# Broadcasting the roots for the keys' normalization in a fused decoder layer: through DRAM in place of a diagonal times ones

## The chip, the cores and the metric

The kernel runs on one core of a Trainium2 chip. The metric is the device time of one execution in microseconds (us), lower is better. A core has five engines with a queue of instructions each: TensorE (PE, matmuls, with its weight loads shown apart as PEld), VectorE (DVE), ScalarE (ACT), GpSimd (POOL) and SyncE (SP), which here only issues DMAs. An engine runs its queue in order and waits for others by semaphores.

## What is computed

One hybrid decoder layer on 1024 tokens with 1024 channels: RMS norm, one projection, sliding-window attention beside retention, an output projection, and a feed-forward part with a convolution. What matters here is the beginning, cut from the reference:

```python
def rms_norm(x, w):
    xf = x.astype(jnp.float32)
    y = xf * lax.rsqrt(jnp.mean(xf * xf, axis=-1, keepdims=True) + RMS_EPS)
    return (y * w.astype(jnp.float32)).astype(x.dtype)
...
        h = rms_norm(x, mix_pre_norm[l])
        proj = jnp.einsum('bsd,de->bse', h, w_in[l])
        q_a, k_a, v_a, q_r, k_r, v_r, g_r = jnp.split(proj, splits, axis=-1)
        attn_out = sliding_window_sink_attention(q_a, k_a, v_a, attn_sinks[l])
        ret_out = retention_group(q_r, k_r, v_r, g_r)
```

The kernel projects the input without dividing it by its root mean square, and brings the factor of each token in afterwards. For most products this factor is a column (tokens lie on partitions). The keys of the attention lie the other way: 128 key channels on the partitions, 512 tokens along the row. For them the factors of 512 tokens are needed as a row, repeated on all 128 partitions.

## The kernel before

The tokens are worked in two halves of 512 (`hh` = 0 and 1). The matmuls take float32 operands as a sum of two reduced parts, `hi` and `lo`: `split` (L114) makes `hi` on ACT (L118, tiles `oh_...`) and `lo` on DVE (L119, tiles `ol_...`), and `mm3` (L125) issues three matmuls for each product: L127 with `hi`, L128 with the other operand's `lo`, L129 with the weights' `lo`. The weights come by `load_w` (L109), a DMA in SP's queue into one of three buffers, so that a load waits until DVE has split the load three before it.

A half begins with `prepare`, which loads and splits the input, and then runs a list of units (L529 to L532): `q_unit` for the four blocks of queries, with `half_sums` between them (loads of the tokens as rows, `mixa` and `mixr`, squared and summed by ACT), `setup`, `k_unit` for the keys, and four `nat_unit` for values. `setup` calls `half_stats`, which computes the roots: a sum on DVE (`v_pre`, L144), the power -1/2 on POOL (`r_pre`, L146), and a few scaled copies on DVE. It then loads constants and tables: in the first half `rm`, `nsink`, `rc`, `cvp`, and in both `cs` and `sn`. In the second half the units stand interleaved with the retention of the first half (tiles `pO`, `pV`, `pI`, `pK`, `inn`, `knat`, `gnt`).

`k_unit` multiplies the keys' weights with the input into `ps_k` (24 matmuls), makes the repeated row `bs`, and multiplies `ps_k` by it into `kn`, which is then split into `kkh` and `kkl`. The row is made in `broadcast`: DVE multiplies the identity by each of the four columns of roots (`diag`, L152), PE multiplies a matrix of ones by that (`bc`, L156, in float32), and ACT copies the result out of PSUM (`bs`, L230).

The order on each engine is set when the program is built, by a scheduler that places instructions by their dependencies and its own estimates; `in_turn` fixes it for a few buffers. A pool hands out buffers in turn by tag: `ttile` is a pool of five (`bs`, `kn`, `sw`, `inn`, `knat`, `gnt`, `th`, `ao` use it), and whoever takes a buffer waits for the last reader of the tile that had it.

Of the kernel before, what the change touches and what calls it, by code (L numbers as in the profile page):

```python
# [8 lines left out]
F32 = mybir.dt.float32  # L9
F32R = mybir.dt.float32r  # L10
AF = mybir.ActivationFunctionType
ALU = mybir.AluOpType
AX = mybir.AxisListType

P = 128
# [12 lines left out]
def tile_hymba_layer(  # L28
# [18 lines left out]
    nc = tc.nc  # L47
# [5 lines left out]
    dr = ctx.enter_context(tc.tile_pool(name="dr", bufs=1, space=bass.MemoryType.DRAM))  # L53
# [4 lines left out]
    def small(name):  # L58
        return pss.tile([P, H], F32, tag="psm", name=name)
# [7 lines left out]
    def xtile(name):  # L67
        return g.tile([P, H], F32, tag="fx", name=name, bufs=2)

    def const(name, shape):  # L70
        return g.tile(shape, F32, tag=name, name=name)

    ident = const("ident", [P, P])
    make_identity(nc, ident)
    ones = const("ones", [P, P])
# [14 lines left out]
    cvp = const("cvp", [P, 2 * NF, 4])  # L90
    nsink = const("nsink", [P, 8])
    rc = const("rc", [P, 3, 4])
    x1d = dr.tile([2, P, D], F32, name="x1d")
    yd = dr.tile([NF, P, D], F32, name="yd")
    ud = dr.tile([EARLY, P, D], F32, name="ud")
# [36 lines left out]
    def block(src, act, name):  # L132
        ops = split_w(src, 1024, H, name) if isinstance(src, bass.AP) else src
        ps = big(f"ps_{name}")
        ah, al = act
        for k in range(8):
            hi, lo = ops[k // 4]
            ks = slice(k % 4 * P, k % 4 * P + P)
            mm3(ps, hi[:, ks], lo[:, ks], ah[k // 4][:, k % 4, :], al[k // 4][:, k % 4, :], k == 0, k == 7)
        return ps  # L140

    def rms(ss, n, name):
        v = g.tile([P, n], F32, tag="cv", name=f"v_{name}", bufs=4)
        nc.vector.tensor_scalar(out=v, in0=ss, scalar1=1.0 / D, scalar2=EPS, op0=ALU.mult, op1=ALU.add)  # L144
        r = g.tile([P, n], F32, tag="cr", name=f"r_{name}", bufs=4)
        nc.gpsimd.tensor_tensor(out=r, in0=v, in1=mhalf[:, :n], op=ALU.pow)  # L146
        return v, r

    def broadcast(r, name):
        diag = xtile(f"diag_{name}")  # L150
        for b in range(4):
            nc.vector.tensor_scalar(  # L152
                out=diag[:, b * P : b * P + P], in0=ident, scalar1=r[:, b : b + 1], scalar2=None, op0=ALU.mult
            )
        bc = small(f"bc_{name}")
        nc.tensor.matmul(bc, ones, diag, start=True, stop=True)  # L156
        return bc


    mixer = ExitStack()  # L160
    m = mixer.enter_context(tc.tile_pool(name="m", bufs=1, reuse_waits="tile"))
# [1 line left out]
    def ttile(name, dt=F32):  # L163
        return m.tile([P, H], dt, tag="t", name=name, bufs=5)
# [3 lines left out]
        out=tri, in_=ones, pattern=[[-1, P]], compare_op=ALU.is_ge, fill=0.0, base=0, channel_multiplier=1  # L168
# [34 lines left out]
    def half_stats(hh, st):  # L203
        ss = st["ss"]
        v, r = rms(ss, 4, f"pre{hh}")
        r8 = m.tile([P, 4], F32, tag="r8", name=f"r8_{hh}", bufs=2)
        nc.vector.tensor_scalar(out=r8, in0=r, scalar1=0.125, scalar2=None, op0=ALU.mult)
        rh = m.tile([P, 4], F32, tag="rh", name=f"rh_{hh}", bufs=2)
        nc.vector.tensor_scalar(out=rh, in0=r, scalar1=0.5, scalar2=None, op0=ALU.mult)
        r2 = m.tile([P, 4], F32, tag="r2", name=f"r2_{hh}", bufs=2)  # L210
        nc.vector.tensor_tensor(out=r2, in0=r, in1=r, op=ALU.mult)
        nr8 = m.tile([P, 4], F32, tag="nr8", name=f"nr8_{hh}", bufs=2)
        nc.vector.tensor_scalar(out=nr8, in0=r, scalar1=-0.125, scalar2=None, op0=ALU.mult)
        return v, r, r8, rh, r2, nr8

    def q_unit(hh, j, act, st):
# [8 lines left out]

    def k_unit(hh, act, st):
        ps = block(w_inT[4], act, f"k{hh}")
        bc = broadcast(st["cols"][1], f"pre{hh}")
        bs = ttile(f"bs{hh}")
        nc.scalar.activation(bs, bc, AF.Copy)  # L230
        kn = ttile(f"kn{hh}")
        nc.vector.tensor_tensor(out=kn, in0=ps, in1=bs, op=ALU.mult)
        cs = slice(P, P + H)
        if hh == 1:
            for t in (kkh, kkl):
                nc.scalar.activation(t[:, :, 0:P], t[:, :, H : H + P].bitcast(F32), AF.Copy)
        for gi in range(2):
            own = slice(gi * 64, gi * 64 + 64)
            oth = slice(64 - gi * 64, 128 - gi * 64)
            for o in (own, oth):  # L240
                nc.scalar.activation(kkh[o, gi, cs], kn[own, :], AF.Copy)
            for o in (own, oth):
                nc.vector.tensor_tensor(
                    out=kkl[o, gi, cs], in0=kn[own, :], in1=kkh[own, gi, cs].bitcast(F32), op=ALU.subtract
                )
# [262 lines left out]
    for hh in range(2):  # L508
        act, w0 = prepare(hh)
        st = dict(w0=w0, q1={}, rq={}, rk={}, va=va_all, vr={}, gp={}, s={}, p={}, ik={}, t={})  # L510
        stages.append(st)
        cs = m.tile([P, H], F32, tag="cs", name=f"cs{hh}")
        sn = m.tile([P, H], F32, tag="sn", name=f"sn{hh}")
        st["rot"] = (cs, sn)
        st["mixa"] = atile(f"mixa{hh}", F32)
        st["mixr"] = atile(f"mixr{hh}", F32)

        def setup(hh=hh, st=st, cs=cs, sn=sn):
            st["cols"] = half_stats(hh, st)
            if hh == 0:  # L520
                nc.sync.dma_start(rm, rmask)
                nc.sync.dma_start(nsink, sinks)
                nc.vector.tensor_scalar(out=nsink, in0=nsink, scalar1=-1.0, scalar2=None, op0=ALU.mult)
                nc.sync.dma_start(rc, rcols)
                nc.sync.dma_start(cvp, convp)
            nc.sync.dma_start(cs, rot[0, hh])
            nc.sync.dma_start(sn, rot[1, hh])

        first = [(q_unit, hh, 0, act, st), (q_unit, hh, 1, act, st), (half_sums, hh, st, (0, 1))]  # L529
        first += [(q_unit, hh, 2, act, st), (half_sums, hh, st, (2, 3)), (q_unit, hh, 3, act, st), (setup,)]  # L530
        first += [(k_unit, hh, act, st)]
        first += [(nat_unit, hh, 0, kk, act, st) for kk in range(4)]  # L532
        interleave(first, prev)
        second = [(rot_unit, hh, t, h, act, st) for t in range(2) for h in range(4)]
        second += [(nat_unit, hh, w, kk, act, st) for w in (1, 2) for kk in range(4)]
        interleave(second, att_stages(hh, st), 0.95)
        prev = ret_stages(hh, st)
# [136 lines left out]
    for hh in range(2):  # L674
        ha, la = split_mix(hh, "mixa", "ma")
        hr, lr = split_mix(hh, "mixr", "mr")
        st = dict(m={})
        st_out.append(st)
        main = [(out_unit, hh, dh, kk, ((ha, hr), (la, lr)), st) for dh in range(2) for kk in range(4)]
        if hh == 0:  # L680
            interleave(main, prev, 0.85)
            mixer.close()
            f = ctx.enter_context(tc.tile_pool(name="ffn", bufs=1, reuse_waits="tile"))
# [536 lines left out]
```

## Time and profile before

| | before |
|---|---|
| runs, median (lowest to highest) | 1061.22 us (1060.53 to 1061.4), 3 runs |
| the profiled execution, its own time | 1060.87 us |
| its span in the trace | 1059.2 us |
| granted TensorE clock, mean | 0.997 |
| instructions | 14259 |
| PE busy | 1047.8 us |
| DVE busy | 820.7 us |
| ACT busy | 592.4 us |
| POOL busy | 111.0 us |
| DMA moved | 149.67 MB |

The span reaches from the first to the last instruction in the trace; what lies around it is 1.7 us. Times in the timelines count from the start of the span. A line names the engine, the line of the kernel, the operation and the tiles, written before read, with the buffers' numbers left out; SPq marks a DMA issue in SP's queue. The sum of busy times is far above the span because the engines work beside each other.

### The profile page before, as it was taken

The page shows a single profiled execution, that of the slowest core. Times are in us where ns is not written, and L with a number is a line of the kernel's source. Part 1 is how long each engine was busy: PE and PEld are TensorE (multiplying, and loading weights), DVE is VectorE, ACT ScalarE, POOL GpSimd, SP SyncE. Part 2 cuts the span into 40 slices and gives each one's busy share as a digit, 9 for nine tenths or more (in the row PEclk, how much of TensorE's full clock was granted, in tenths as well). Part 3 has the DMA queues.
Part 4 walks back from the last instruction along what each step waited for, and adds up shares of the span by engine and source line. Part 5 has one row for each costly group of instructions (what it writes and reads, how often), then busy time and mean ns, then how long its engine had stood idle before and what let it go on. Part 6 is the DMA issues. An engine that isn't in the chain of part 4 may idle for free.

```text
span 1059.2 us, 14259 instructions
## 1 busy us (share of the span) xinstructions
PE 1047.8 (99%) x5004; PEld 887.9 (84%) x5004; DVE 820.7 (77%) x1416; ACT 592.4 (56%) x1140; POOL 111.0 (10%) x135
## 2 busy tenths in 40 slices
PE   9999999999999999999999999999999999999996
PEld 7988998988998888888888888888888888888885
DVE  5567777667686685987787888978879898858695
ACT  7566772466662567665555455555555545445461
POOL 1013332124322110000000000000000000000032
PEclk9999999999999999999999999999999999999998
DMA  8322541222231473864423234233233695604576
GB/s 317 114 80 68 172 174 46 95 80 61 65 108 53 166 251 107 297 213 149 139 86 123 100 110 139 95 114 113 97 140 109 239 338 173 231 33 163 180 195 118
DMA packets 53928, 149.67 MB, mean 141 GB/s; under 512 B 6368, under 2 KB 6496, under 8 KB 53856
## 3 DMA queue, kind: packets, MB, share of 16 engines
q1 hardware_dynamic: 51840, 145.09, 39.8%
q0 software_dynamic: 1728, 3.15, 2.0%
q8 instruction: 39, 0.64, 0.2%
q10 hardware_dynamic: 288, 0.52, 0.1%
q14 instruction: 33, 0.27, 0.1%
HBM read 123.05 MB, written 25.69 MB: 140 GB/s over the span
## 4 chain that ended last, share of the span: by engine, by line
issue 57%; PE 37%; DVE 2%; POOL 1%; DMA 1%; ACT 1%; DVEq 0%; POOLq 0%; ACTq 0%
PE pn L129 3%; PE pn L127 3%; PE pn L128 3%; PE ps_r L127 3%; PE ps_r L128 3%; PE ps_r L129 3%; PE po L127 2%; PE po L129 2%; PE po L128 2%; PE ps_q L128 1%; PE ps_q L129 1%; PE ps_q L127 1%; PE pS L319 1%; PE pS L318 1%; PE pI L395 1%
## 5 line engine op out<-in xcount | busy, mean ns | idle before, releaser
L127 PE MATMUL pd<-oh_d,sh_d 128*128 128x512 f32 x264 | 103.8, 393 | 0.0
L128 PE MATMUL pd<-ol_d,sh_d 128*128 128x512 f32 x264 | 103.2, 391 | 0.0
L129 PE MATMUL pd<-oh_d,sl_d 128*128 128x512 f32 x264 | 103.0, 390 | 0.0
L710 DVE SCALAR_TENSOR_TENSOR a<-uv,cvp,a 128x1023 f32<-128x1023 f32 (+1 forms) x44 | 56.2, 1278 | 22.1 <-ACT a L707 22.1
L1013 POOL TENSOR_TENSOR fs<-fs,mhalf 128x1 f32<-128x1 f32 x8 | 8.3, 1039 | 594.0 <-DVE fs L1010 594.0
L127 PE MATMUL pn<-oh_n,xh 128*128 128x384 f32 x192 | 65.9, 343 | 0.0
L129 PE MATMUL pn<-oh_n,xl 128*128 128x384 f32 x192 | 64.4, 336 | 0.0
L128 PE MATMUL pn<-ol_n,xh 128*128 128x384 f32 x192 | 64.3, 335 | 0.0
L129 PEld LDWEIGHTS pd<-oh_d,sl_d 128*128 128x128 f32 x264 | 49.6, 188 | 11.3
L127 PEld LDWEIGHTS pd<-oh_d,sh_d 128*128 128x128 f32 x264 | 49.6, 188 | 10.9 <-DVE ug L872 0.2
L128 PEld LDWEIGHTS pd<-ol_d,sh_d 128*128 128x128 f32 x264 | 49.6, 188 | 10.4
L710 DVE SCALAR_TENSOR_TENSOR a<-ug,cvp,a 128x1023 f32<-128x1023 f32 (+1 forms) x44 | 56.3, 1279 | 1.2 <-ACT a L707 1.1
L127 PE MATMUL ps_r<-xh,oh_r 128*128 128x512 f32 x128 | 50.6, 396 | 0.0
L128 PE MATMUL ps_r<-xl,oh_r 128*128 128x512 f32 x128 | 50.0, 391 | 0.0
L129 PE MATMUL ps_r<-xh,ol_r 128*128 128x512 f32 x128 | 50.0, 390 | 0.0
L336 ACT ACTIVATE s<-s,sc,r 128x128 f32<-128x128 f32 x64 | 30.9, 483 | 30.2 <-DVE sc L330 30.2
L118 ACT ACTIVATE oh_n<-wr_n 128x384 fp32r<-128x384 f32 x48 | 24.2, 521 | 30.0 <-PE ps_q L128 8.6
L118 ACT ACTIVATE oh_o<-wr_o 128x512 fp32r<-128x512 f32 x32 | 20.0, 635 | 34.2 <-PE po L129 32.9
L707 ACT ACTIVATE a<-ug,cvp 128x1024 f32<-128x1024 f32 x22 | 27.3, 1241 | 19.3 <-DVE ug L872 15.3
L744 DVE TENSOR_TENSOR raw<-raw 128x512 f32<-128x512 f32 x22 | 15.2, 689 | 28.4 <-DMA raw<-w_u 28.4
L718 ACT ACTIVATE sh_d<-r 128x512 fp32r<-128x512 f32 x33 | 20.7, 629 | 28.6 <-PE pd L128 21.9
L119 DVE TENSOR_TENSOR ol_o<-wr_o,oh_o 128x512 fp32r<-128x512 f32 x32 | 23.1, 732 | 17.3 <-ACT oh_o L118 17.2
(1248 smaller groups left out, 3289.0 us busy)
## 6 DMA issues: line engine op xcount, KB each, us to landing
raw<-w_u SPq DMA_DIRECT2D x44, 512.0 KB, 4.4
yd<-a SPq DMA_DIRECT2D x22, 512.0 KB, 2.9
r<-yd SPq DMA_DIRECT2D x22, 512.0 KB, 5.5
wr_n<-w_inN SPq DMA_DIRECT2D x24, 384.0 KB, 3.1
wr_r<-w_inT SPq DMA_DIRECT2D x16, 512.0 KB, 3.4
wr_o<-w_o SPq DMA_DIRECT2D x16, 512.0 KB, 3.4
wr_e<-w_u SPq DMA_DIRECT2D x11, 512.0 KB, 4.4
ud<-e SPq DMA_DIRECT2D x11, 512.0 KB, 3.9
```

Of the source, the lines that this page charges most:

```text
L118: in_turn("oh", nc.scalar.activation(hi[:, :n], src, AF.Copy))
L119: nc.vector.tensor_tensor(out=lo[:, :n], in0=src, in1=hi[:, :n].bitcast(F32), op=ALU.subtract)
L127: ins = nc.tensor.matmul(ps, lh, rh, start=first, stop=False, skip_group_check=onto)
L128: nc.tensor.matmul(ps, lh, rl, start=False, stop=False, skip_group_check=onto)
L129: nc.tensor.matmul(ps, ll, rh, start=False, stop=end, skip_group_check=onto)
L318: nc.tensor.matmul(ps[:, i, :nk], lq, kkh[:, gi, k0 : k0 + nk], start=True, stop=False)
L319: nc.tensor.matmul(ps[:, i, :nk], lq, kkl[:, gi, k0 : k0 + nk], start=False, stop=True)
L336: nc.scalar.activation(s[:, i, :], s[:, i, :], AF.Exp, scale=r8, bias=c[:, 1, i : i + 1], accum_out=c[:, 3, i : i + 1])
L707: nc.scalar.activation(a, u[:, c0 : c0 + n], AF.Identity, scale=cvp[:, b, 2:3], bias=cvp[:, b, 3:4])
L710: nc.vector.scalar_tensor_tensor(out=a[:, s:], in0=u[:, c0 + s - d : c0 + n - d], scalar=cvp[:, b, tap : tap + 1], in1=a[:, s:], op0=ALU.m ...
L718: in_turn("sh", nc.scalar.activation(hi, src, AF.Copy))
L744: nc.vector.tensor_tensor(out=a11, in0=a11, in1=a21, op=ALU.subtract)
```

## The change

The repeated row is no longer made by DVE, PE and ACT. `half_stats` sends the roots (128 partitions with 4 columns each) to a new DRAM tile `rd` by a DMA that writes element by element, so that `rd` holds 4 x 128 numbers in the tokens' order, and a second DMA reads these 512 numbers back to each of the 128 partitions, into `bs`. Both are issued from SP. The second waits until the first has landed. `broadcast` goes, with its matrix product; `k_unit` takes `bs` as it finds it. `bs` is taken from the pool of five earlier, in `setup`.

```diff
@@ -90,6 +90,7 @@
     rc = const("rc", [P, 3, 4])
+    rd = dr.tile([2, 4, P], F32, name="rd")
     x1d = dr.tile([2, P, D], F32, name="x1d")
@@ -145,16 +146,6 @@
-    def broadcast(r, name):
-        diag = xtile(f"diag_{name}")
-        for b in range(4):
-            nc.vector.tensor_scalar(
-                out=diag[:, b * P : b * P + P], in0=ident, scalar1=r[:, b : b + 1], scalar2=None, op0=ALU.mult
-            )
-        bc = small(f"bc_{name}")
-        nc.tensor.matmul(bc, ones, diag, start=True, stop=True)
-        return bc
@@ -211,6 +202,9 @@
         nc.vector.tensor_scalar(out=nr8, in0=r, scalar1=-0.125, scalar2=None, op0=ALU.mult)
+        nc.sync.dma_start(rd[hh].rearrange("b p -> p b"), r)
+        st["bs"] = ttile(f"bs{hh}")
+        nc.sync.dma_start(st["bs"], rd[hh].rearrange("b p -> (b p)").partition_broadcast(P))
         return v, r, r8, rh, r2, nr8
@@ -225,9 +219,7 @@
         ps = block(w_inT[4], act, f"k{hh}")
-        bc = broadcast(st["cols"][1], f"pre{hh}")
-        bs = ttile(f"bs{hh}")
-        nc.scalar.activation(bs, bc, AF.Copy)
+        bs = st["bs"]
         kn = ttile(f"kn{hh}")
```

What the scheduler makes of it is seen in the order of instructions. SP's queue in the first half, before (loads of constants and tables, then of the weights of the keys, `wr_k`, and of the values, `wr_n`):

```order
L524 DMA rc<-rcols 128x12
L525 DMA cvp<-convp 128x176
L526 DMA cs_153<-rot 128x512
L527 DMA sn_154<-rot 128x512
L112 DMA wr_k_339<-w_inT 128x1024
L112 DMA wr_n_0_0_397<-w_inN 128x768
```

and now:

```order
L516 DMA rc<-rcols 128x12
L205 DMA rd<-r_pre_323 128x4x1
L517 DMA cvp<-convp 128x176
L518 DMA cs_154<-rot 128x512
L519 DMA sn_155<-rot 128x512
L207 DMA bs_334<-rd 128x512
L113 DMA wr_k_343<-w_inT 128x1024
L113 DMA wr_n_0_0_392<-w_inN 128x768
```

The write of the roots stands ahead of three loads, and the read back ahead of `wr_k`; nothing else in this stretch of the queue has changed its place.

SP's queue in the second half, at the same units, before:

```order
L200 DMA mixr_1622<-xN 128x1024 x2
L112 DMA wr_k_1968<-w_inT 128x1024
L112 DMA wr_n_0_0_2042<-w_inN 128x768
L112 DMA wr_n_0_1_2082<-w_inN 128x768
L112 DMA wr_n_0_2_2155<-w_inN 128x768
L112 DMA wr_n_0_3_2195<-w_inN 128x768
```

and now:

```order
L191 DMA mixr_1617<-xN 128x1024 x2
L113 DMA wr_k_1966<-w_inT 128x1024
L113 DMA wr_n_0_0_2031<-w_inN 128x768
L205 DMA rd<-r_pre_1912 128x4x1
L113 DMA wr_n_0_1_2071<-w_inN 128x768
L113 DMA wr_n_0_2_2144<-w_inN 128x768
L207 DMA bs_1923<-rd 128x512
L113 DMA wr_n_0_3_2184<-w_inN 128x768
```

Here both stand behind `wr_k`, among the loads for the values.

PE at the end of the keys' block in the first half, before (`ps_k` keys, `bc` the product of ones and the diagonal, `pn` values):

```order
L127 MATMUL ps_k_349<-xh_1_111,oh_k_512_345 128x512
L128 MATMUL ps_k_349<-xl_1_113,oh_k_512_345 128x512
L129 MATMUL ps_k_349<-xh_1_111,ol_k_512_346 128x512
L156 MATMUL bc_pre_379<-diag_pre_374,ones 128x512
L127 MATMUL pn_0_0_393<-oh_n_0_0_0_399,xh_0_110 128x384
L128 MATMUL pn_0_0_393<-ol_n_0_0_0_400,xh_0_110 128x384
```

and now:

```order
L128 MATMUL ps_k_353<-xh_1_112,oh_k_512_349 128x512
L129 MATMUL ps_k_353<-xl_1_114,oh_k_512_349 128x512
L130 MATMUL ps_k_353<-xh_1_112,ol_k_512_350 128x512
L128 MATMUL pn_0_0_388<-oh_n_0_0_0_394,xh_0_111 128x384
L129 MATMUL pn_0_0_388<-ol_n_0_0_0_395,xh_0_111 128x384
```

The values follow the keys directly. The rest of PE's queue is as it was, but for the same product in the second half, which stood ahead of `pI` of block 3.

## The prediction

> **What bounds the kernel now.** I read the busy shares of the page first, then the busy time by stretches, then the waits of TensorE, and last the timelines of single engines around the two places where the change acts. The page's first part says that PE is the bound.
>
> ```profile
> PE 1047.8 (99%) x5004; PEld 887.9 (84%) x5004; DVE 820.7 (77%) x1416; ACT 592.4 (56%) x1140; POOL 111.0 (10%) x135
> ```
>
> A busy PE need not be a full PE, so the stretches come next (columns: microseconds, then busy time of each engine with its instructions, granted clock, DMA share, GB/s). The removed work lies between 29 and 36 us (first half, hh=0) and between 150 and 190 us (second half, hh=1).
>
> ```profile
> 29.00:36.00 7.00, 7.00 (x31) 5.54 (x30) 3.75 (x7) 2.96 (x6) 0.00 (x0) 1.00 0.57 188
> 150.00:186.00 36.00, 36.00 (x213) 31.61 (x212) 27.04 (x82) 14.97 (x28) 6.74 (x7) 1.00 0.25 91
> 186.00:190.00 4.00, 4.00 (x26) 3.52 (x25) 3.71 (x6) 2.62 (x5) 1.32 (x1) 1.00 0.40 131
> ```
>
> PE is busy in every microsecond of them at a granted clock of 1.00. The view of waits, for PE alone, agrees:
>
> ```profile
> PE hot L89 <- DVE mhalf L78: 1.1, 1, 1.1
> PE ps_q L128 <- DVE xl L188: 0.6, 2, 0.3
> PE pR L466 <- POOL gnt L459: 0.2, 1, 0.2
> ```
>
> In 1059.2 us PE waits for others 1.9 us. So a slot of PE that goes is worth its length, a new wait of PE costs its length, and DVE, ACT and the queues matter only where they make PE wait.
>
> **What is removed.** Per half one float32 matmul `bc` (L156), four DVE products `diag` (L152) and one ACT copy `bs` (L230). The slot of `bc` is read from PE's timeline (start, duration, instruction). First half:
>
> ```profile
> 34.62 1.02 PE L156 MATMUL bc_pre<-diag_pre,ones 128*128 128x512 f32 x2
> 35.08 0.74 PE L127 MATMUL pn<-oh_n,xh 128*128 128x384 f32 x1
> 35.66 0.34 PE L128 MATMUL pn<-ol_n,xh 128*128 128x384 f32 x1
> 35.84 0.33 PE L129 MATMUL pn<-oh_n,xl 128*128 128x384 f32 x1
> ```
>
> Durations overlap, so I count from starts. `pn` matmuls follow each other by 0.18 us (35.66 to 35.84). The first `pn` has a record of 0.74 us because it stands behind `bc`; its own slot begins 0.18 us before the second, at 35.48. The slot of `bc` is 34.62 to 35.48, **0.86 us**. Second half:
>
> ```profile
> 185.90 1.02 PE L156 MATMUL bc_pre<-diag_pre,ones 128*128 128x512 f32 x2
> 186.76 1.05 PE L395 MATMUL pI<-rq,rq 128*128 128x128 f32 x8
> ```
>
> Again 186.76 - 185.90 = 0.86 us. Together **-1.72 us**. DVE and ACT get their work back too, but PE does not wait for either engine in these stretches, so I count it at nothing. The chain from `ps_k` to `kn` gets shorter: `kn` no longer waits for `bc` and its copy, and what reads it comes later.
>
> **What is added, second half.** Two DMAs stand in SP's queue: `rd` (the roots, out to DRAM) between `wr_n_0_0` and `wr_n_0_1`, and `bs` (the broadcast back) between `wr_n_0_2` and `wr_n_0_3`. SP issued those four loads here:
>
> ```profile
> 152.18 0.33 SPq L112 DMA_DIRECT2D wr_n<-w_inN  x1
> 159.34 0.33 SPq L112 DMA_DIRECT2D wr_n<-w_inN  x1
> 168.50 0.33 SPq L112 DMA_DIRECT2D wr_n<-w_inN  x1
> 177.49 0.33 SPq L112 DMA_DIRECT2D wr_n<-w_inN  x1
> ```
>
> The roots come from POOL, and the buffer that `bs` takes is the one that `pO` of block 1 reads:
>
> ```profile
> 156.89 1.02 POOL L146 TENSOR_TENSOR r_pre<-v_pre,mhalf 128x4 f32<-128x4 f32 x1 [12.16 <-DVE v_pre L144]
> ```
>
> ```profile
> 169.36 0.39 PE L420 MATMUL pO<-S,rq 128*128 128x128 f32 x2
> 169.59 0.50 PE L425 MATMUL pV<-vr,knat 128*128 128x128 f32 x3
> ```
>
> `rd` can go at 157.9, while SP waits anyway until 159.34. `bs` can go at about 169.8, SP has nothing else until 177.49, and `kn`, its reader, needs `ps_k`, which ends at about 185.9. Even a landing of 8 us is hidden; without that cover it would cost what it exceeds. So: nothing.
>
> **What is added, first half.** Here `rd` stands between `rc` and `cvp`, and `bs` between `sn` and `wr_k`. SP's issues before the change, and POOL's root:
>
> ```profile
> 12.96 0.33 SPq L524 DMA_DIRECT2D rc<-rcols  x1
> 14.16 0.33 SPq L525 DMA_DIRECT2D cvp<-convp  x1
> 15.43 0.33 SPq L526 DMA_DIRECT2D cs<-rot  x1
> 16.70 0.33 SPq L527 DMA_DIRECT2D sn<-rot  x1
> 17.99 0.33 SPq L112 DMA_DIRECT2D wr_k<-w_inT  x1
> 19.24 10.82 SPq L112 DMA_DIRECT2D wr_n<-w_inN  x4
> ```
>
> ```profile
> 21.02 1.03 POOL L146 TENSOR_TENSOR r_pre<-v_pre,mhalf 128x4 f32<-128x4 f32 x1 [18.48 <-DVE v_pre L144]
> ```
>
> Before, `wr_k` was issued at 17.99, long before the roots exist. Now SP stands at `rd` until the roots are there, at 22.05, and everything queued behind it waits: `cvp`, `cs`, `sn`, `bs`, `wr_k`, and then the four `wr_n`. SP stands a second time at `bs`, until `rd` has landed. Only then does it reach `wr_k`, which ACT and DVE split and PE needs next:
>
> ```profile
> 26.74 1.15 ACT L118 ACTIVATE oh_k<-wr_k 128x512 fp32r<-128x512 f32 x2
> ```
>
> ```profile
> 27.47 0.69 DVE L119 TENSOR_TENSOR ol_k<-wr_k,oh_k 128x512 fp32r<-128x512 f32 x1
> ```
>
> ```profile
> 29.18 0.39 PE L127 MATMUL ps_k<-xh,oh_k 128*128 128x512 f32 x1
> ...
> 29.63 0.39 PE L129 MATMUL ps_k<-xh,ol_k 128*128 128x512 f32 x1
> ```
>
> From the start of `oh_k` to the end of the first `ol_k` is 27.47 + 0.69 - 26.74 = 1.42 us, and PE's third matmul of `ps_k`, at 29.63, is the first that needs `ol_k`. So `wr_k` must have landed by 29.63 - 1.42 = **28.21**, or PE waits. No row shows `rd` or a DMA like it, so its landing is bounded. The view of DMA issues (size, median us to landing) has:
>
> ```profile
> wr_r<-w_inT SPq DMA_DIRECT2D x16, 512.0 KB, 3.4
> ...
> ug<-ud SPq DMA_DIRECT2D x11, 256.0 KB, 2.5
> ...
> gn<-gains SPq DMA_DIRECT2D x1, 4.0 KB, 3.7
> ...
> ```
>
> and the shortest landing of a store that I found is that of the rows of `outN`:
>
> ```profile
> DMA to landing us min/median/max: 2.0/4.0/6.3
> ```
>
> `rd` moves 2 KB as 512 elements of 4 bytes, into queues that are nearly empty by then. Below: 2.0 us. Above: `gn`, 128 short rows, needs 1.7 us more than that; if that excess is all per row, four times the rows give 2.0 + 4 x 1.7 = 8.8 us. I take **3.1 us**, between `ug` (2.5, an unhurried queue) and `gn` (3.7, small pieces behind one load at the start), the rows to which it is nearest.
>
> The spacing of SP's free issues is 0.46 us:
>
> ```profile
> 0.81 0.39 SPq L81 DMA_DIRECT2D xr<-xT  x1
> 1.25 0.42 SPq L84 DMA_DIRECT2D gn<-gains  x1
> 1.72 0.42 SPq L183 DMA_DIRECT2D xr<-xT  x1
> ```
>
> So `rd` is issued at 22.1 and lands at 25.2; `cvp`, `cs` and `sn` go out meanwhile, by 23.9. `bs` follows at 25.2, `wr_k` at 25.66. It lands after 3.4 us like `wr_r`, plus 0.25 us (estimate: 256 KB of `bs` at the 415 GB/s of the next row take 0.63 us, of which 0.46 have gone by, and I round up).
>
> ```profile
> 20.00:22.00 2.00, 2.00 (x11) 1.65 (x10) 0.57 (x2) 1.95 (x5) 0.98 (x1) 1.00 1.04 415
> ```
>
> Landing at 29.31 is 1.10 us past 28.21: PE waits **+1.10 us**. The `wr_n` loads behind it are needed from `pn` on, about 5.4 us after `ps_k` begins (29.18 to 34.62), and are issued directly after `wr_k`; they stay covered. At the low end (2.0, and `wr_k` after 3.1) it lands by 28.0 and the wait is nothing; at the high end (8.8) it is 6.8 us. That all 128 partitions of `bs` read the same 2 KB of DRAM is shown by no row either: below, it costs nothing more than a load of its size; above, I take what the slowest `ug` (5.6 against 2.5 us) would add, 3.1 us.
>
> [...]
>
> **The sum**: -0.86 - 0.86 + 1.10 = -0.62 us. Against the profiled execution's own 1060.87 us that is 1060.25; it lies 0.35 us under the median of the runs shown, 1061.22, so on that scale **1060.6 us**.
>
> **Rivals.** 0.2%, about what a measurement of this kernel can tell from no change, is 2.1 us.
>
> *The trip is short* (30 in 100): `rd` lands in 2.0 us, `wr_k` is in time, and only the removed slots count: 1061.2 - 1.7 = 1059.5 us. For it: the least `outN` and the empty queue. It still is within 0.2%. Faster by over 0.2% needs some further 0.4 us, for which I see no row.
>
> *The trip is long, and SP's queue is what pays* (18): `rd` is 512 single elements, 32 for each of 16 DMA engines, and lands late; SP stands at `bs`, `wr_k` comes late, and PE stands before `ps_k`. Each microsecond of landing beyond 2.0 is a microsecond of PE. The kernel is slower than before from a wait of 1.72 us, a landing of 3.7 us, and slower by over 0.2% from a wait of 3.84 us, a landing of 5.8 us. At 8.8 us it is 1061.2 - 1.7 + 6.8 = 1066.3 us. A slow `bs` works at the same place. For it: `gn` needs 3.7 us for only 128 pieces. Against: its start is also the kernel's start. [...]
>
> *The forecast* (52): a wait between the two, net -1.7 to +2.1.
>
> **Chances and range.** Faster by over 0.2%: 0.04 (the short trip plus something unseen). Slower: 0.18, the long trip. Within: the rest, 0.78. The range goes from the short trip less the 0.4 us by which the runs scatter, 1059.1, to the upper bound of `rd`, 1066.3.
>
> **What would show it.** In the changed profile SP's `rd` starts at about 22.1 and `wr_k` at 25.7; PE shows a new wait for `oh_k` or `ol_k` of about 1.1 us before or within the first three matmuls of the first `ps_k`; `rd` lands in about 3 us; `pn` follows `ps_k` at once in the first half and `pI` in the second; nothing waits for `bs`. I am wrong if PE stands for `wr_n` or `kn`, if the second half has a new wait, or if the roots come at another time than 22.05.

## The result, and the profile after

| | before | after |
|---|---|---|
| runs, median (lowest to highest) | 1060.76 us (1060.53 to 1061.4), 6 runs | 1070.06 us (1068.79 to 1070.77), 6 runs |
| the profiled execution | 1060.87 us | 1069.22 us |
| its span | 1059.2 us | 1067.5 us |
| mean granted TensorE clock | 0.997 | 0.994 |
| instructions | 14259 | 14250 |

The ratio of after to before is 1.0086, with a 95% interval of 1.0076 to 1.0096: the kernel is 9 us slower. The forecast was 1060.6 us with a range up to 1066.3, so the time lies outside it, on the side of the rival "the trip is long".

In the page's first part PE has lost the four instructions of the two removed products (5004 before; each product stands as x2 in its timeline), and its busy time has still not fallen:

```profile
PE 1048.1 (98%) x5000; PEld 889.1 (83%) x5000; DVE 818.7 (77%) x1408; ACT 591.1 (55%) x1138; POOL 110.7 (10%) x135
```

The view of PE's waits names the place. One wait is new; the others were there before, some 0.1 us longer or shorter:

```profile
PE ps_k L128 <- ACT oh_k L119: 9.5, 1, 9.5
```

`oh_k` is the split of `wr_k`, so the question is where that load was. SP's timeline of the first half (start, duration, instruction):

```profile
22.39 0.38 SPq L205 DMA_DIRECT2D rd<-r_pre  x1
22.82 0.50 SPq L517 DMA_DIRECT2D cvp<-convp  x1
23.36 0.43 SPq L518 DMA_DIRECT2D cs<-rot  x1
23.84 0.43 SPq L519 DMA_DIRECT2D sn<-rot  x1
31.44 0.33 SPq L207 DMA_DIRECT2D bs<-rd  x1
31.86 0.38 SPq L113 DMA_DIRECT2D wr_k<-w_inT  x1
```

and the DMA issues of the stretch from 15 to 60 us (KB of one, median us from issue to landing), where each of these occurs once:

```profile
wr_k<-w_inT SPq DMA_DIRECT2D x1, 512.0 KB, 6.5
cs<-rot SPq DMA_DIRECT2D x1, 256.0 KB, 11.1
sn<-rot SPq DMA_DIRECT2D x1, 256.0 KB, 11.6
bs<-rd SPq DMA_DIRECT2D x1, 256.0 KB, 5.6
cvp<-convp SPq DMA_DIRECT2D x1, 88.0 KB, 8.7
rd<-r_pre SPq DMA_DIRECT2D x1, 2.0 KB, 9.0
```

`rd`, 2 KB, takes 9.0 us, and SP stands at `bs` until 31.44. But not `rd` alone is late: `cvp`, `cs` and `sn`, issued right behind it and waiting for nothing, take 8.7 to 11.6 us. The stretches show PE standing and the DMA engines moving next to nothing until 32 us, and then everything at once (columns as before: busy times, clock, DMA share, GB/s):

```profile
28.00:30.00 2.00, 1.70 (x8) 1.09 (x6) 0.00 (x0) 0.00 (x0) 0.00 (x0) 1.00 0.24 35
30.00:32.00 2.00, 0.00 (x0) 0.00 (x0) 0.00 (x0) 0.00 (x0) 0.00 (x0) 1.00 0.35 25
32.00:34.00 2.00, 0.00 (x0) 0.00 (x0) 0.00 (x0) 0.00 (x0) 0.00 (x0) 0.84 0.36 101
34.00:36.00 2.00, 0.00 (x0) 0.00 (x0) 0.00 (x0) 0.00 (x0) 0.00 (x0) 0.50 0.98 191
36.00:38.00 2.00, 0.00 (x0) 0.00 (x0) 0.00 (x0) 0.00 (x0) 0.00 (x0) 0.50 0.97 356
```

The clock column (the third from the right) has a second loss that the waits don't show: while PE stands, its granted clock falls to 0.50. PE's timeline has what that costs:

```profile
39.17 0.80 PE L128 MATMUL ps_k<-xh,oh_k 128*128 128x512 f32 x1 [9.47 <-ACT oh_k L119]
39.77 0.63 PE L129 MATMUL ps_k<-xl,oh_k 128*128 128x512 f32 x1
40.19 0.63 PE L130 MATMUL ps_k<-xh,ol_k 128*128 128x512 f32 x1
...
43.85 0.39 PE L130 MATMUL ps_k<-xh,ol_k 128*128 128x512 f32 x1
44.08 0.39 PE L128 MATMUL ps_k<-xh,oh_k 128*128 128x512 f32 x1
...
46.82 0.33 PE L128 MATMUL pn<-oh_n,xh 128*128 128x384 f32 x1
```

The matmuls of `ps_k` start 0.42 us apart until the clock is back, then 0.23. All 24 take 46.82 - 39.17 = 7.65 us. Before they took 34.62 - 29.18 = 5.44, so they are 2.21 us slower; that is half of the 4.43 us from 39.17 to 43.60, in which the next matmul started 0.42 us after the last. The account up to the first `pn`, which began at 35.48 in before: the wait 9.47, the clock 2.21, the removed slot -0.86, and 0.52 because PE came to the end of `ps_q` later in this execution (39.17 - 9.47 = 29.70, against 29.18). The sum is 11.34, and 46.82 - 35.48 = 11.34.

In the second half SP issues both DMAs as thought, and PE gets no new wait:

```profile
169.29 0.38 SPq L205 DMA_DIRECT2D rd<-r_pre  x1
...
182.01 0.33 SPq L207 DMA_DIRECT2D bs<-rd  x1
```

The last `pn` of the mixer starts at 313.7 us against 303.2 in before, 10.5 us later: the second slot of 0.86 us is there. By the end the distance of the spans is 8.3 us. The 2.2 us between come in two parts. Some 0.9 us are gained at three places, where `po` turns to `mah` and where `PC` and `pd` begin (near 388, 835 and 843 us in before): PE's last matmul starts 9.6 us later than in before (1059.14 against 1049.56). The other 1.3 lie behind that matmul, in the last outputs, which take 9.6 us in the profiled execution of before and 8.4 in that of after.

### The profile page after: what moved, and what is told of

It is laid out like the page before. It is cut to its first block, busy times and chain, and to the rows that moved or that the text cites. A ratio compares the mean times of both kernels' runs of the same rounds, so it can differ in the third digit from the quotient of the medians.

```text
span 1067.5 us, 14250 instructions
## 1 busy us (share of the span) xinstructions
PE 1048.1 (98%) x5000; PEld 889.1 (83%) x5000; DVE 818.7 (77%) x1408; ACT 591.1 (55%) x1138; POOL 110.7 (10%) x135
## 4 chain that ended last, share of the span: by engine, by line
issue 57%; PE 35%; ACT 2%; DMA 2%; DVE 2%; POOL 1%; SPq 0%; DVEq 0%; POOLq 0%; ACTq 0%
PE pn L128 3%; PE pn L130 3%; PE pn L129 3%; PE ps_r L128 3%; PE ps_r L130 3%; PE ps_r L129 3%; PE po L130 2%; PE po L128 2%; PE po L129 2%; DMA rd<-r_pre 1%; PE ps_q L129 1%; PE ps_q L130 1%; PE ps_q L128 1%; PE pS L311 1%; PE pS L310 1%
## 5 line engine op out<-in xcount | busy, mean ns | idle before, releaser
L129 PEld LDWEIGHTS pd<-ol_d,sh_d 128*128 128x128 f32 x264 | 49.6, 188 | 10.5
L129 PEld LDWEIGHTS pn<-ol_n,xh 128*128 128x128 f32 x192 | 36.1, 188 | 0.1
L128 PEld LDWEIGHTS pn<-oh_n,xh 128*128 128x128 f32 x192 | 36.1, 188 | 0.1
```

The source lines that it names most:

```text
L128: ins = nc.tensor.matmul(ps, lh, rh, start=first, stop=False, skip_group_check=onto)
L129: nc.tensor.matmul(ps, lh, rl, start=False, stop=False, skip_group_check=onto)
```

## Experiments

Two theories stood after the result. **SP's stand**: `rd` lands late because it is 512 pieces, SP stands at `bs` for it, and `wr_k` behind that pays. **The held transfers**: the write itself keeps back whatever stands behind it in the queues, whether SP waits or not. The median of before on the same chip was 1061.17 us for the first four kernels, 1060.69 for the next eight, 1060.93 for the last three. A kernel without an interval was run once.

### The two DMAs elsewhere: e1_pool and e2_late

e1 issues both from POOL:

```diff
-        nc.sync.dma_start(rd[hh].rearrange("b p -> p b"), r)
+        nc.gpsimd.dma_start(rd[hh].rearrange("b p -> p b"), r)
-        nc.sync.dma_start(st["bs"], rd[hh].rearrange("b p -> (b p)").partition_broadcast(P))
+        nc.gpsimd.dma_start(st["bs"], rd[hh].rearrange("b p -> (b p)").partition_broadcast(P))
```

> Both new DMAs are issued from POOL in place of SP; all else as in the changed kernel. Theory (the write of the roots is slow, about 9 us, and only SP's order makes that cost anything): wr_k is issued at about 18 us again, PE does not wait for oh_k, the clock stays at 1.0, the two slots of bc are gone: about 1.7 us below before, near 1059. Rival A (512 four-byte writes hold up the DMA engines for whoever uses them): the weights that are issued after 22 us land late and PE waits by several us for pn, so slower than before. Rival B (the read back, 128 partitions from one 2 KB row, is what is slow): kn comes late and PE stands at the fourth pn, near 38 us.

e2 moves them from `half_stats` into `k_unit`; in SP's queue they then stand behind `wr_k`, among the loads `wr_n`:

```diff
         ps = block(w_inT[4], act, f"k{hh}")
-        bs = st["bs"]
+        nc.sync.dma_start(rd[hh].rearrange("b p -> p b"), st["cols"][1])
+        bs = ttile(f"bs{hh}")
+        nc.sync.dma_start(bs, rd[hh].rearrange("b p -> (b p)").partition_broadcast(P))
```

> The two DMAs stay on SP but are written in k_unit, behind the load of the keys' weights: SP's queue is wr_k, rd, wr_n_0_0, wr_n_0_1, bs. Theory: wr_k is issued at about 18 us, no wait for oh_k, no drop of the clock; wr_n_0_0 goes out at about 23 us and lands behind rd at 31 to 33 us, in time for pn at 34.7; bs lands at about 35 and kn follows within 1 us: near 1059, as the version on POOL. Rival A (the write holds up the engines well beyond its own landing): wr_n_0_0 lands after 34 us and PE waits there, 1060 to 1064.

e1: 1062.32 us, ratio 1.0007 (0.9999 to 1.0016); its profiled execution took 1060.63. e2: 1061.65 us, ratio 1.0004 (0.9996 to 1.0013). In both `wr_k` is issued ahead of the write (18.26 and 18.50 us), and the wait for `oh_k` is gone. But `rd` is no faster there, 10.4 and 11.6 us, and what comes behind it is late: the loads `wr_n`, which ACT splits. DMA issues, PE's waits and ACT's timeline of e1:

```profile
wr_n<-w_inN SPq DMA_DIRECT2D x4, 384.0 KB, 9.5
...
rd<-r_pre POOLq DMA_DIRECT2D x1, 2.0 KB, 10.4
```

```profile
PE pn L128 <- DVE q L217: 1.7, 1, 1.7
```

```profile
36.83 0.52 ACT L119 ACTIVATE oh_n<-wr_n 128x384 fp32r<-128x384 f32 x1 [6.64 <-DMA wr_n<-w_inN]
```

In before the four `wr_n` take 3.3 us (median). Here they take 9.5, though they stand in SP's queue and the write in POOL's; from 26 to 28 us the DMA engines move 6 GB/s. ACT waits 6.6 us for them, the copies `q` stand behind that split, and PE gets its buffer for `pn` late. In e2 the four `wr_n`, two right behind the write and two behind `bs`, take 8.6 us in the median and up to 13.0, ACT waits 8.5 us, and PE waits 1.4 us for `oh_n` and 0.4 for `q`. So taking both transfers out of `wr_k`'s way saves the 9 us and leaves no gain. The long landing is what is to be explained, and e1 already shows it holding loads of another engine's queue.

### Does SP's stand matter? e3_write_only and e4_read_only

e3 is the kernel before with the write added. Nothing reads it, so nothing waits for its landing:

```diff
+    rd = dr.tile([2, 4, P], F32, name="rd")
...
+        nc.sync.dma_start(rd[hh].rearrange("b p -> p b"), r)
```

> The kernel before, with the write of the roots added at its place in the changed kernel and nothing that reads it; the roots are still broadcast by the product. SP stands until the roots are there (22.4 us) but not until the write has landed, so wr_k is issued at about 24.3 us. Theory with the semaphore alone (what costs is SP's stand at the read back): wr_k lands after some 4.5 us like other loads in a row, near 28.8, PE waits about 0.5 us, total within 1 us of before. Theory with held engines: the 512 small writes delay what is queued behind them on the same DMA engines, wr_k lands at 32 to 34 us, PE waits 4 to 6 us, the clock drops for a while, and the kernel is 4 to 8 us slower than before.

1072.58 us, ratio 1.011 (1.0095 to 1.0126): as slow as the whole change and more. SP's timeline and the DMA issues of the same stretch, of e3:

```profile
24.05 0.38 SPq L113 DMA_DIRECT2D wr_k<-w_inT  x1
```

```profile
wr_k<-w_inT SPq DMA_DIRECT2D x1, 512.0 KB, 14.2
...
rd<-r_pre SPq DMA_DIRECT2D x1, 2.0 KB, 9.8
```

```profile
PE ps_k L128 <- ACT oh_k L119: 9.6, 1, 9.6
```

SP reaches `wr_k` at 24.05, 7.8 us earlier than in the kernel after. It lands at 38.3 all the same (after: 31.86 + 6.5 = 38.4), and PE waits 9.6 us. So the loss doesn't need SP's stand; the write alone holds back the loads behind it, and of the two theories the second is enough. What the stand would cost without the hold is not shown: no run has a late `rd` that lets the loads behind it through.

e4 is the kernel after without the write; `bs` is read from an input, so that the read stays and its wait goes:

```diff
-        nc.sync.dma_start(rd[hh].rearrange("b p -> p b"), r)
-        nc.sync.dma_start(st["bs"], rd[hh].rearrange("b p -> (b p)").partition_broadcast(P))
+        nc.sync.dma_start(st["bs"], wides[0][0, 0:H].partition_broadcast(P))
```

> The changed kernel without the write: bs is read to all partitions from a row of an input, 512 numbers that are not the roots, and waits for nothing. Every theory that puts the loss on the write or on SP's order expects the removed slots alone here: about 1.7 us below before, near 1059, no wait of PE at ps_k. If the read of one 2 KB row by 128 partitions were the cost, bs would land after more than 6 us and the loads behind it late, with a wait of PE in the first 30 us.

1058.19 us, ratio 0.9973 (0.9964 to 0.9983). PE waits for nothing at `ps_k`. The first `pn` starts at 34.6 (35.48 in before), the last at 301.4 (303.2): the two slots of 0.86 us are worth what they were counted at. Of the rest of the 3.0 us, some 0.7 come at the same three places as in the kernel after (388, 835 and 843 us), and in e7 and e8 too; no wait explains them, and their cause is open.

### What makes the write slow? e6, e9, e10, e14, e15

All five are e3 with the 512 numbers laid out otherwise; still nothing reads them. The tile and the write of each:

```diff
 e3   rd = dr.tile([2, 4, P], ...)       dma_start(rd[hh].rearrange("b p -> p b"), r)
 e6   rd = dr.tile([2, 4, P, 128], ...)  dma_start(rd[hh, :, :, 0].rearrange("b p -> p b"), r)
 e10  rd = dr.tile([2, 4, P, 16], ...)   as e6
 e15  rd = dr.tile([2, 4, P, 4], ...)    as e6
 e14  rd = dr.tile([2, 4, P, 2], ...)    as e6
 e9   rd = dr.tile([2, P, 4, 2], ...)    dma_start(rd[hh, :, :, 0], r)
```

> As the kernel with the write alone (the product still broadcasts the roots), but each of the 512 numbers goes to a place of its own, 512 bytes apart, in a larger DRAM tile. If the price is per piece, rd lands in 9 to 10 us and wr_k in about 14, as there, with a wait of PE of over 9 us. If it comes from 16 DMA engines writing into the same few lines of DRAM, rd lands in 2 to 4 us, wr_k in 4 to 6, and PE waits under 2 us.

> The kernel before plus the write of the roots, which nothing reads; the 512 numbers lie column by column, 64 bytes from one another. Theory A (what collides is a stretch of 64 bytes or less): the write lands in about 2 us as with 512 bytes between the numbers, no wait for oh_k, about 1060 to 1061 us. Theory B (what collides is a stretch of some 512 bytes): it lands in 6 to 10 us and PE waits 5 to 10 us for oh_k, 1066 to 1073 us.

> The kernel before plus the write of the roots, which nothing reads; here the 512 numbers lie token by token, every one as a piece of its own, 8 bytes from its neighbour, so that the four numbers of one partition lie in 32 bytes together. Theory A (the cost comes from several DMA engines writing into the same short stretch of DRAM, the partitions being spread over the engines): fewer engines meet in a stretch than when the numbers lay column by column, so the write lands in under 4 us, wr_k in under 7 us, no wait for oh_k, about 1060 to 1061 us. Theory B (the cost comes from many small pieces packed into a few KB, whichever engine writes them): the write lands in 8 to 10 us, PE waits 7 to 10 us for oh_k, 1069 to 1073 us. A landing between 4 and 8 us would mean that neighbours of different partitions still meet.

> The kernel before plus the write of the roots, which nothing reads; the numbers lie column by column, 8 bytes from one another: 8 of them, of 8 partitions, in 64 bytes. Theory A (the cost goes with the number of pieces in a stretch of 64 bytes, some 0.55 us each: 16 pieces 9.0 to 10, 8 pieces 4.3): it lands in 4 to 5 us and PE waits 2 to 3 us for oh_k, about 1063 to 1066 us. Theory B (the cost goes with the number of partitions that meet there, 16 in the packed layout and 2 in the one with tokens together): it lands in 6 to 9 us, PE waits 4 to 8 us.

> The kernel before plus the write of the roots, which nothing reads; the numbers lie column by column, 16 bytes from one another: 4 of them, of 4 partitions, in 64 bytes. Theory A (0.55 us for each piece in a stretch of 64 bytes, and never under some 2 us): it lands in 2 to 3 us, PE waits under 1.5 us for oh_k, about 1061 to 1063 us. Theory B (the number of partitions that meet): it lands in more than the 4.3 us that were measured with 2 partitions in a stretch, and PE waits over 2.5 us.

| | bytes between numbers | numbers in 64 bytes | of so many partitions | `rd` lands in (and in the second half) | `wr_k` lands in | PE waits for `oh_k` | time |
|---|---|---|---|---|---|---|---|
| e3 | 4 | 16 | 16 | 9.8 us (10.0) | 14.2 us | 9.6 us | 1072.58 |
| e14 | 8 | 8 | 8 | 3.8 (5.0) | 7.0 | 2.5 | 1065.16 |
| e9 | 8, four of a partition together | 8 | 2 | 4.3 (5.5) | 6.7 | 2.5 | 1065.6 |
| e15 | 16 | 4 | 4 | 3.2 (2.9) | 5.4 | 0.8 | 1062.51 |
| e10 | 64 | 1 | 1 | 2.1 (2.0) | 5.0 | 0.4 | 1062.11 |
| e6 | 512 | 1 | 1 | 2.1 (1.8) | 4.7 | none | 1060.78 |

Every row moves the same 512 pieces of 4 bytes from the same place in the queue. With 512 bytes between them the write takes 2.1 us and the loads behind it flow; the DMA issues and the stretches of e6:

```profile
wr_k<-w_inT SPq DMA_DIRECT2D x1, 512.0 KB, 4.7
...
rd<-r_pre SPq DMA_DIRECT2D x1, 2.0 KB, 2.1
```

```profile
24.00:26.00 2.00, 2.00 (x11) 1.65 (x10) 1.97 (x7) 0.52 (x1) 0.00 (x0) 1.00 0.85 244
26.00:28.00 2.00, 2.00 (x10) 1.69 (x9) 0.75 (x2) 0.59 (x1) 0.00 (x0) 1.00 0.98 349
```

and the same stretches of e3, with the same loads queued:

```profile
24.00:26.00 2.00, 2.00 (x10) 1.67 (x9) 1.97 (x7) 0.54 (x1) 0.00 (x0) 1.00 0.04 14
26.00:28.00 2.00, 2.00 (x10) 1.67 (x9) 0.78 (x2) 0.59 (x1) 0.00 (x0) 1.00 0.19 31
```

The row of `rd` in e10, with 64 bytes between the numbers:

```profile
rd<-r_pre SPq DMA_DIRECT2D x1, 2.0 KB, 2.1
```

So it is not a price per piece, as the prediction's upper bound had it. It is the packing: the landing falls with the number of pieces that lie in 64 bytes, in both halves, from 9.8 and 10.0 us with 16 of them to 2.1 and 2.0 with one, and 512 bytes between them make it no shorter in the first half (2.1 us) and 0.2 us in the second (1.8). e9 and e14 have eight pieces in 64 bytes from two and from eight partitions and land alike (4.3 and 3.8 us), and e15, with four partitions in a stretch, is faster than e9 with two. So it is not the number of partitions that meet. e9's first theory (a landing under 4 us and no wait) was missed. (Times of one execution scatter by about 1 us; the landings and waits carry the argument.)

Two things stay open. The first is the length of the stretch. These layouts thin out every stretch at once, longer ones too, and nothing between 16 and 64 bytes was tried: 64 is the shortest distance tried at which the landing was 2.1 us, and not a measured grain. Nor is it a fixed price for each piece in 64 bytes, as e14 and e15 expected (0.55 us): from four pieces to eight the landing grows by 0.6 to 1.1 us, from eight to 16 by 5.5 to 6.0. The rival in e10, a stretch of some 512 bytes, falls: by it pieces 64 bytes apart would still be in one another's way, and they landed in 2.1 us, as with 512 bytes. The second is what happens to the pieces. In the kernel after, where the write is issued at 22.39 us, the view of DMA from 22.9 to 23.7 us counts

```profile
DMA packets 528, 0.00 MB, mean 3 GB/s; under 512 B 528, under 2 KB 528, under 8 KB 528
```

The 512 pieces are among them; the trace has all 528 at 7 to 9 ns each, from 23.30 to 23.68 us. `rd` landed at 31.4 (22.39 + 9.0), so 7.7 us of its 9.0 lie behind these records. What happens in those 7.7 us no run shows.

### Larger pieces, in three places: e5, e7, e8

With `rd` as tokens by columns, the four numbers of a partition make one piece of 16 bytes. `kn` reads `bs` with a stride in return:

```diff
-    rd = dr.tile([2, 4, P], F32, name="rd")
+    rd = dr.tile([2, P, 4], F32, name="rd")
...
-        nc.sync.dma_start(rd[hh].rearrange("b p -> p b"), r)
+        nc.sync.dma_start(rd[hh], r)
...
-        nc.vector.tensor_tensor(out=kn, in0=ps, in1=bs, op=ALU.mult)
+        nc.vector.tensor_tensor(
+            out=kn.rearrange("q (b p) -> q b p", b=4), in0=ps.rearrange("q (b p) -> q b p", b=4),
+            in1=bs.rearrange("q (p b) -> q b p", b=4), op=ALU.mult,
+        )
```

e5 does this in the places of the change, e7 with both DMAs on POOL as in e1, e8 with both behind `wr_k` as in e2.

> The changed kernel at the same places of SP's queue, but the roots go out as they lie: 128 pieces of 16 bytes in place of 512 of 4, and kn reads bs with a stride that puts the order right. If the price is per piece: (9.0 - 2.0) / 512 is 14 ns each, 128 of them land in about 3.8 us, wr_k is issued near 26.7 and lands at 31 to 33, PE waits 2.5 to 4.5 us for oh_k, the clock hardly drops, the kernel is 1 to 3 us slower than before. If a small store costs some 9 us whatever its number of pieces, it stays at about 1070.

> 128 pieces of 16 bytes, and both DMAs issued from POOL. By the price per piece rd lands in about 5 us (POOL's own took 10.6 against 9.0 on SP), near 27.5, bs at 32 to 33, before ps_k is done at 34.6: no wait of PE but those of the start, the slots of bc gone, and the weights behind are held for a short while only. 1.7 to 3 us below before (the kernel without the write was 3.0 below). If even this write holds the engines for 9 us, PE waits 1 to 2 us for pn as in the version on POOL with 512 pieces, and the time is that of before.

> 128 pieces of 16 bytes on SP, written behind the load of the keys' weights (wr_k, rd, wr_n_0_0, wr_n_0_1, bs). By the price per piece rd lands near 26.5, wr_n_0_0 by 30, bs near 31: no wait of PE at pn, 1.7 to 3 us below before. If the write holds the engines for 9 us again, PE waits about 2 us at pn as in the version with 512 pieces.

| | `rd` lands in (and in the second half) | PE's new wait | median (lowest to highest) | ratio |
|---|---|---|---|---|
| e5 | 1.4 us (3.4) | `oh_k` 2.2 us | 1062.52 us (1061.36 to 1062.87) | 1.0015 (1.0006 to 1.0024) |
| e7 | 3.2 (2.1) | none | 1058.06 (1057.53 to 1058.69) | 0.9975 (0.9965 to 0.9984) |
| e8 | 1.8 (3.5) | none | 1057.94 (1057.28 to 1058.51) | 0.9974 (0.9964 to 0.9983) |

With four pieces in 64 bytes, as in e15 (3.2 and 2.9 us), the write takes 1.4 to 3.5 us. e5's theory of a price per piece (3.8 us) was missed.

e8 and e7 beat both kernels, by 2.8 and 2.6 us against before. The step from e2 to e8, and from e1 to e7, is the layout alone, with the stride that it brings into `kn`: the ratio falls by 0.0030 and 0.0032, or 3.2 and 3.4 us. The DMA issues of e8 show the trip that the change needs, 1.8 + 4.3 us, all behind `wr_k`:

```profile
wr_k<-w_inT SPq DMA_DIRECT2D x1, 512.0 KB, 4.7
...
bs<-rd SPq DMA_DIRECT2D x1, 256.0 KB, 4.3
rd<-r_pre SPq DMA_DIRECT2D x1, 2.0 KB, 1.8
```

e5 has the fast write in the change's own places and still pays, because there `wr_k` goes out at 25.25 behind four other loads and lands after 6.3 us. Its DMA issues and two stretches:

```profile
wr_k<-w_inT SPq DMA_DIRECT2D x1, 512.0 KB, 6.3
...
bs<-rd SPq DMA_DIRECT2D x1, 256.0 KB, 5.5
```

```profile
28.00:30.00 2.00, 2.00 (x10) 1.49 (x8) 0.00 (x0) 0.00 (x0) 0.00 (x0) 1.00 0.99 217
30.00:32.00 2.00, 0.18 (x1) 0.00 (x0) 0.00 (x0) 0.33 (x1) 0.00 (x0) 1.00 1.00 408
```

### Is the repeated row slow to read? e12_own_rows

The 217 GB/s at a full DMA share made the read of one row by 128 partitions suspect. e12 is e5 with `bs` filled from 128 rows of an input:

```diff
-        nc.sync.dma_start(st["bs"], rd[hh].rearrange("p b -> (p b)").partition_broadcast(P))
+        nc.gpsimd.tensor_copy(st["bs"][:, 0:4], r)
+        nc.sync.dma_start(st["bs"], wides[0][:, 0:H])
```

> As the kernel with pieces of 16 bytes on SP in the places of the change, but bs is filled from 128 different rows of an input of 2 KB each, in place of one row of roots for all partitions (the keys are scaled by wrong numbers; POOL writes four columns of bs first, so that the DMA still waits for the roots). Theory (128 partitions that read one row of DRAM are slow, and hold up wr_k): bs lands in about 3 us in place of 5.5, wr_k in about 4.7 in place of 6.3, PE waits under 1 us in place of 2.2 for oh_k, about 1060.5 to 1061.5 us. Rival (bs costs what any 256 KB cost there): bs lands in over 5 us, wr_k in over 6, the wait stays at 2 us or more, 1062 to 1063 us.

1061.34 us, ratio 1.0005 (0.9995 to 1.0015). The DMA issues and PE's wait of e12:

```profile
wr_k<-w_inT SPq DMA_DIRECT2D x1, 512.0 KB, 6.1
bs<-wides SPq DMA_DIRECT2D x1, 256.0 KB, 5.2
```

```profile
PE ps_k L128 <- ACT oh_k L119: 1.9, 1, 1.9
```

The theory falls for the larger part: `bs` is 0.3 us faster, `wr_k` 0.2, the wait 0.3. `bs` costs nearly what 256 KB from separate rows cost there. What makes `wr_k` late in e5 and e12 is, at least in part, company: in e6, where the same loads stand without `bs`, it is issued at 24.02 and lands in 4.7 us, 1.6 us sooner than in e5. `cvp`, `cs`, `sn`, `bs` and `wr_k` are 88 + 3 x 256 + 512 = 1368 KB, and at the 408 GB/s of the full stretch that is 3.4 us of transfer; why only 217 GB/s are moved before that stretch is open. (SP's order differs a little: in e12 `bs` goes ahead of `cvp`.)

### What the halved clock is worth: e11_warm and e13_warm8

Both are the kernel after with float32 matmuls on PE, ahead of the first `ps_k`, whose result nobody uses, ten in e11 and eight in e13:

```diff
+        if hh == 0:
+            fill = small("fill")
+            for _ in range(10):
+                nc.tensor.matmul(fill, ones, rm.rearrange("p h q -> p (h q)"), start=True, stop=True)
         ps = block(w_inT[4], act, f"k{hh}")
```

> The kernel after with ten float32 matmuls of 512 columns more, whose result nobody uses, on PE between the last ps_q and the first ps_k, some 8.6 us of work in the place where PE stood idle for 9.5 us. Theory (PE loses about 2.0 us more than its wait, because its clock is halved after the idle time): the granted clock stays at 1.0, the wait for oh_k falls to about 1 us, the 24 matmuls of ps_k take 5.4 to 5.6 us instead of 7.65, and the time is about 2 us below that of the kernel after, 1068 us. Rival (the slow matmuls of ps_k come from the DMA traffic or from late operands, not from the idle PE): the clock or the pitch of ps_k is as slow as without the extra matmuls, and the time is that of the kernel after, 1070 us, or more.

> The kernel after with eight float32 matmuls of 512 columns more on PE between the last ps_q and the first ps_k (6.9 us, in place of ten). Theory (the halved clock costs some 2 us, and the later landing with ten matmuls was chance): the granted clock stays at 1.00, the 24 matmuls of ps_k take 5.4 to 5.9 us, wr_k lands near 38.4 us as in the kernel after, and the ratio to the kernel before is about 1.007. Rival (matmuls in that place, or a warm PE, make the landing late, so that the clock is worth nothing): wr_k lands near 40 us again and the ratio is 1.0085 or more.

e11: 1070.37 us, ratio 1.0092 (1.0077 to 1.0107). e13: 1071.41 us, ratio 1.0102 (1.0085 to 1.0119). PE's timeline of e11:

```profile
29.56 8.75 PE L224 MATMUL fill<-rm,ones 128*128 128x512 f32 x20
40.92 0.50 PE L128 MATMUL ps_k<-xh,oh_k 128*128 128x512 f32 x1 [2.60 <-ACT oh_k L119]
...
46.80 0.33 PE L128 MATMUL pn<-oh_n,xh 128*128 128x384 f32 x1
```

The price of the clock is shown: at a granted clock of 1.00 the 24 matmuls of `ps_k` take 46.80 - 40.92 = 5.88 us in place of 7.65, with the same late loads around them. That is 1.77 us less and not 2.21, because the third matmul now stands for the split `ol_k` (41.25 to 41.64). That the clock stayed up was luck of the moment, as the last section shows. The time did not fall, because `rd` took 10.6 us in this execution and `ps_k` began 1.75 us later. In e13 `rd` took 10.6 us again, PE stood 4.0 us, and the clock fell to 0.50 after all, so e13's theory was missed, and the numbers are those of its rival. But the added matmuls are not what makes `rd` late: in the second half, where there are none, it took 10.3 and 10.6 us in e11 and e13, and in e1, e2 and e3, which have none at all, 9.8 to 11.6 in both halves. The 9.0 and 8.9 us of the kernel after are the shortest that were measured with this layout, and neither e11 nor e13 came out shorter than the kernel after.

## Why the prediction was wrong

Point by point, by its own steps:

- **PE is the bound, and a new wait of PE costs its length.** Right as a lower bound, and incomplete: the wait of 9.47 us cost 11.7 (9.47 + 2.21), because the clock fell to 0.50. The sum had no term for that. It is 2.21 us in the kernel after, of which e11 wins 1.77 back.
- **The two slots, -1.72 us.** Right. e4, e7 and e8, where no wait covers them, have the last `pn` 1.6 to 1.8 us earlier. They are up to 3.0 us faster in all; 0.7 to 0.9 us of that appears between 303 us and PE's last matmul, at the same three places as in the kernel after, which the change doesn't touch. No cause was found.
- **The second half adds nothing.** Right: both DMAs stood where they were put by the order, `rd` took 8.9 us there too, and nothing waited.
- **`rd` lands in 3.1 us, between 2.0 and 8.8.** This is the step that failed. It landed in 9.0, and 9.8 to 11.6 in other kernels that write it in the same layout. The value was taken by nearness to loads of whole rows. The same view of before had two small loads, of 4 and 6 KB, that took 8.3 and 7.3 us (`nsink`, `rc`, issued behind larger ones), and the prediction passed over them. The upper bound came out near the truth for a wrong reason: it was built as a price for each of 512 pieces, and 512 pieces take 2.1 us when they lie apart (e6, e10). What costs is that they lie packed, 16 of them in 64 bytes (9.8 us in e3).
- **SP stands at `bs`, and `wr_k` pays for it.** The stand is in the trace, from 24.3 to 31.44, and puts `wr_k` 6.2 us later than forecast, but it isn't needed: without it (e3) `wr_k` landed at the same time, held by the write. The prediction has no hold, and neither has the rival "the trip is long", which named the right symptom. It follows that the cures differ: sparing SP the stand while `wr_k` is behind `rd` saves nothing (e3), putting `wr_k` ahead of `rd` does (e2).
- **`wr_k` lands in 3.65 us.** It took 6.5. The 3.4 us were those of `wr_r`; `wr_k` itself took 4.8 us in the first half of before. The prediction let `cvp`, `cs` and `sn` be done by then. They were held with the rest, and all five loads moved together from 32 us on. Even with a fast write they meet: 6.3 in e5.
- **The upper end of the range, 1066.3 us.** It held a landing of 8.8 us and nothing else late. The missing terms, 2.85 us of `wr_k` and 2.2 us of clock, were each visible as a question: the slow `bs` "at the same place" had been priced at up to 3.1 us and was then left out of the end of the range.

The account of the whole: the wait 9.47, the clock 2.21, the two slots -1.72, the later end of `ps_q` 0.52; these are 10.48 us. The spans differ by 8.3. Between lie -0.9 at the three places near 388, 835 and 843 us, where the cause is open, and -1.3 behind PE's last matmul, where before took 9.6 us in its one profiled execution and after 8.4.

## What to carry to other kernels

The 2 KB write of this case was priced neither by its bytes nor by its pieces: the same 512 pieces of 4 bytes landed in 9.8 us side by side (e3), in 3.2 at 16 bytes apart (e15) and in 2.1 at 64 (e10). So look at how densely the pieces of a small transfer lie in DRAM, and put a scattered write behind the loads that matter, since what was issued after it was held even without a wait (e3, `wr_k` landed in 14.2 us) and from another queue (e1, `wr_n` in 9.5 us). A version that gained (e8, 2.8 us) did both, with 128 pieces of 16 bytes in place of 512 of 4. When a wait of PE is estimated at two microseconds or more, count with one or more stretches of 3.4 us at half clock behind it: one followed the wait of 2.2 us in e5, three that of 9.5 us in the kernel after, none that of 2.6 us in e11.

## What the runs showed of the hardware that was not expected

**A 2 KB write held back 1.1 MB of loads in its own queue, and loads in another engine's.** In e3 the engines moved 14 and 31 GB/s from 24 to 28 us with `cvp`, `cs`, `sn` and `wr_k` queued (88 + 2 x 256 + 512 KB), and the recorded busy share of the engines was 0.04 and 0.19. In e1, with the write in POOL's queue and `wr_n` in SP's, they moved 32 and 6 GB/s. The busy share doesn't tell a hold: in e1 it was 0.88 from 24 to 26 us, while the 32 GB/s were moved.

**In these runs the clock fell and rose in steps of 3.4 us, and a wait of 1.9 us was enough.** Half-microsecond stretches of the kernel after, at the fall, at the rise and at the next fall:

```profile
33.00:33.50 0.50, 0.00 (x0) 0.00 (x0) 0.00 (x0) 0.00 (x0) 0.00 (x0) 0.86 0.42 66
...
43.50:44.00 0.50, 0.50 (x3) 0.35 (x3) 0.03 (x1) 0.00 (x0) 0.00 (x0) 0.90 0.99 307
...
1064.00:1064.50 0.50, 0.00 (x0) 0.00 (x0) 0.04 (x1) 0.00 (x0) 0.00 (x0) 0.69 0.87 336
```

and of e5:

```profile
32.00:32.50 0.50, 0.15 (x1) 0.15 (x1) 0.17 (x1) 0.50 (x2) 0.00 (x0) 0.85 1.05 424
...
35.50:36.00 0.50, 0.50 (x3) 0.45 (x2) 0.50 (x1) 0.00 (x0) 0.00 (x0) 0.73 0.98 393
```

A mean of 0.86 between 1.00 and 0.50 puts the fall at 0.72 of the stretch, 33.36, and 0.90 puts the rise at 43.60: 10.24 us, or 3 x 3.413. The same reading of 0.69 puts the next fall at 1064.19, 1020.59 us after the rise, or 299 x 3.4133. In e5 the clock is down from 32.35 to 35.77, 3.42 us, one step. It fell after waits of 1.9 us (e12), 2.2 (e5) and 2.5 (e9, e14). It didn't fall after 1.7 (e1), nor after 2.6 (e11), so the length of a wait doesn't decide alone. How much of it falls into one step fits all of these. In e11 the clock next falls at the end of the span:

```profile
1063.00:1063.50 0.50, 0.00 (x0) 0.00 (x0) 0.50 (x2) 0.00 (x0) 0.00 (x0) 0.84 1.12 229
```

That is at 1063.34, and 300 steps of 3.4133 us, the length from the kernel after, before it another step ends, at 39.34. It cuts the wait, which ends at 40.92, into 1.0 and 1.6 us. The waits of e5 and e12 lie whole in the step that ends with the fall, from 28.94 to 32.35 and from 29.49 to 32.90. So a step with 1.9 us or more of standing was followed by one at half clock (1.9 in e12, 2.2 in e5, 3.4 in the kernel after), and one with 1.6 (e11) or at most 1.7 (e1) was not; where between them it turns, and whether that holds elsewhere, is not shown. What one such fall costs is an estimate: about 1.7 us, half of 3.42, when PE works through it. In the kernel after it was 2.21 us for the 4.43 us that PE worked through.
